# Low parts of the mixer's weights computed during the first feed-forward block and kept in DRAM

## The chip, the core and the metric

The kernel runs on one core of one Trainium2 chip. The metric is the device time of one execution in microseconds (us).

## The reference, cut to what matters

One layer of a decoder for 512 prompt tokens and 8 x 4 sample tokens, model width 1024: a feed-forward half step, a mixer, a second feed-forward half step, each followed by a layer norm.

```python
h = layer_norm(ALPHA * x + 0.5 * swiglu(x, ffn1_w_gate, ffn1_w_up, ffn1_w_down), ln1_g, ln1_b)
mixed, state = mix_fn(h, lw)            # projections by w_in, two head groups, projection by w_out
h = layer_norm(ALPHA * h + mixed, ln2_g, ln2_b)
y = layer_norm(ALPHA * h + 0.5 * swiglu(h, ffn2_w_gate, ffn2_w_up, ffn2_w_down), ln3_g, ln3_b)
```

swiglu(x) is (silu(x @ w_gate) * (x @ w_up)) @ w_down with a hidden width of 2816. The mixer's head groups are a state-space scan (SSD) and an attention with a compressed, a selected and a window branch. All of it is float32.

## The kernel before, in words

Every large matmul is made of three with fewer bits: a float32 operand is split into a high part (the value rounded to the type fp32r) and a low part (the value minus the high part), and `gemm` (lines 256 to 265) adds high x high, high x low and low x high in PSUM. Activations are split once, when they are made (`split`, lines 190 to 192). Weights are split each time they are used, by the class `Weights` (lines 149 to 172).

The weights are cut into units, mostly 128 x 8 x 128 values (512 KB; 128 partitions of 4 KB). The list `units` holds them in the order of use: 44 gate and up units and 24 down units of the first feed-forward block, the mixer's, then the second block's. `Weights.load` (line 160) issues a load of the next unit into `w_raw` (2 buffers) on SP's queue. `Weights.get` makes `w_hi` on ScalarE (line 170) and `w_lo` on VectorE, or on POOL where the caller says so (line 171); both have 3 buffers, so a unit's buffers are free when TensorE has finished with the unit three before it.

The mixer has 33 units: 20 projections of `w_in` (kc, vc, ks, kw, vs, vw, q0 to q3, x0 to x5, z0 to z3), one narrow one for dt and gates (`wdg`, 128 x 8 x 32), four of the key and value compression (c0 to c3) and eight of `w_out` (`wout`). The four c units are used twice, for the prompt and for the samples, so `get` is called 37 times in the mixer. The callers are `proj` (line 618 on; POOL makes the low part, except for kc), `compress_prompt` (POOL), `compress_sample` (VectorE) and the output projection in `mix` (`attention(d)`, VectorE). In the output projection the attention half of unit d+3 follows the other half of unit d.

The two feed-forward blocks are calls of one function, `ffn` (from line 367). For each of 22 f it takes a gate and a up unit, two token halves of 272 columns each, SiLU on ScalarE, the product on VectorE and a split of the product into hH and hL; then for each of 8 d it takes three down units, and VectorE, ScalarE and POOL make the residual and the sums for the norm (lines 272, 307 to 326, 421).

The order of each engine's queue is planned when the program is built, `tile.TileContext(nc, schedule_with_timeline_sim=True)`: the program's text gives ranks, and the planner follows a simulated time line and puts next into a queue what is ready then. On the chip each engine, and SP and POOL as issuers of DMAs, then runs its queue in that fixed order, waiting where something is late.

Of the kernel before, what the change touches and what calls it, by code (L numbers as in the profile page):

```python
# [25 lines left out]
F32 = mybir.dt.float32  # L26
F32R = mybir.dt.float32r
BF = mybir.dt.bfloat16
I32 = mybir.dt.int32
AF = mybir.ActivationFunctionType  # L30
OP = mybir.AluOpType
# [5 lines left out]
D, KD = 1024, 8  # L37
# [111 lines left out]
class Weights:  # L149


    def __init__(self, nc, pool, units, dma):
        self.nc, self.pool, self.units, self.dma, self.n = nc, pool, units, dma, 0
        self.raw = []

    def load(self):
        ap = self.units[self.n + len(self.raw)]
        _, nk, m = ap.shape
        raw = self.pool.tile([128, 8, 128], F32, name="w_raw", bufs=2)
        self.dma.dma_start(raw[:, :nk, :m], ap)  # L160
        self.raw.append(raw)

    def get(self, eng=None, pool=None):
        if not self.raw:
            self.load()
        nc, raw = self.nc, self.raw.pop(0)
        _, nk, m = self.units[self.n].shape
        self.n += 1
        hi, lo = ((pool or self.pool).tile([128, 8, 128], F32R, name=n, bufs=1 if pool else 3) for n in ("w_hi", "w_lo"))
        nc.scalar.activation(hi[:, :nk, :m], raw[:, :nk, :m], AF.Copy)  # L170
        (eng or nc.vector).tensor_tensor(lo[:, :nk, :m], raw[:, :nk, :m], hi.bitcast(F32)[:, :nk, :m], op=OP.subtract)  # L171
        return hi, lo


@with_exitstack
def step_kernel(ctx, tc, I, O, stop=99):
# [40 lines left out]

    ffn_units("1")
    seen = []
    for step in T0_ORDER + T1_ORDER + T2_ORDER:  # L220
        if step in ("c0", "c1", "c2", "c3"):
            units.append(I["w1"][int(step[1])])
        elif step == "dg":
            units.append(I["wdg"])
        elif step == "k" and seen.count("k") < 2:
            units.extend([I["w1"][seen.count("k") * 2 + i] for i in range(2)])
        elif step == "x":
            units.append(I["win"][IN_TILES.index(f"x{seen.count('x')}")])
        elif step in IN_TILES:
            units.append(I["win"][IN_TILES.index(step)])  # L230
        seen.append(step)
    units.extend([I["wout"][d] for d in range(KD)])
    ffn_units("2")
    W = Weights(nc, wpool, units, nc.sync)

    with tc.tile_pool(name="xload", bufs=1) as xp:

# [40 lines left out]
    class Norm:  # L278
# [3 lines left out]
        def __init__(self, pool, g, b, n, eps, to_x=True):  # L282
            self.g, self.b, self.eps, self.to_x = g, b, eps, to_x
            self.n = n
            self.m0 = pool.tile([128, 2, HT], F32, name="ln_m0")
            self.accS = keep.tile([128, 2, HT], F32, name=f"accS{n}", tag="accS")
            self.accQ = keep.tile([128, 2, HT], F32, name=f"accQ{n}", tag="accQ")
            self.y, self.rest = [], []
            self.extra_done = False
# [77 lines left out]
    def ffn(pre, post, last):  # L367

        with tc.tile_pool(name="ffn", bufs=1) as fp, tc.tile_pool(name="ffn_ps", bufs=1, space=PS) as pp:
            hH = fp.tile([128, KF, 2, HT], F32R, name="hH")  # L370
            hL = fp.tile([128, KF, 2, HT], F32R, name="hL")
            with tc.tile_pool(name="ffn_g", bufs=1) as gp:
                for f in range(KF):
                    sg = {}
                    for which in range(2):
                        wt = W.get()
                        cw = gp.tile([128, 2], F32, name="cw", bufs=4)
                        for h in range(2):
                            ps = pp.tile([128, 512], F32, name="mm", bufs=6)
                            rh, rl, n = xcols(h, pre is not None)  # L380
                            gemm(ps[:, :n], wt, (rh, rl), KD)
                            if f == 0 and which == 0 and h == 0 and pre is not None:
                                pre.stats(gp, pp)
                            if pre is None:
                                src = ps[:, :HT]
                            else:
                                src = gp.tile([128, HT], F32, name="fold_o", bufs=2)
                                pre.fold(ps, h, cw, src, gp)
                            if which == 0:
                                sg[h] = gp.tile([128, HT], F32, name="sg", bufs=3)  # L390
                                if pre is None:
                                    nc.scalar.activation(sg[h], src, AF.Silu)
                                else:
                                    nc.scalar.activation(sg[h], src, AF.Silu, bias=cw[:, 1:2])
                            else:
                                hf = gp.tile([128, HT], F32, name="hf", bufs=2)
                                if pre is None:
                                    nc.vector.tensor_tensor(hf, src, sg[h], op=MUL)
                                else:
                                    nc.vector.scalar_tensor_tensor(hf, src, cw[:, 1:2], sg[h], op0=ADD, op1=MUL)  # L400
                                split(hH[:, f, h], hL[:, f, h], hf)
            with tc.tile_pool(name="ffn_d", bufs=1) as dp:
                nrm = Norm(dp, *post, eps4, to_x=not last)

                tab = dp.tile([128, 1], F32, name="tab")
                nc.scalar.activation(tab, f32(hH)[:, KF - 1, 1, 0:1], AF.Sqrt, scale=0.0, bias=eps1)
                for d in range(KD):
                    t = dp.tile([128, 2, HT], F32, name="res", bufs=2)
                    if pre is None:
                        padd(t, f32(XH[d])[:, :, :HT], f32(XL[d])[:, :, :HT])  # L410
                    else:
                        pre.value(d, t, dp, nc.gpsimd)
                    ps = [pp.tile([128, 512], F32, name="mm", bufs=6) for _ in range(2)]
                    wts = [W.get() for _ in range(3)]

                    def down(i, h):
                        gemm(ps[h][:, :HT], wts[i], (lambda k: hH[:, k, h], lambda k: hL[:, k, h]),
                             min(8, KF - 8 * i), 8 * i, start=i == 0, stop=i == 2)

                    def residual(h):  # L420
                        nc.vector.scalar_tensor_tensor(t[:, h], t[:, h], 2.0 * ALPHA, ps[h][:, :HT],
                                                       op0=MUL, op1=ADD)

                    if d < KD - 1:
                        for i in range(3):
                            for h in range(2):
                                down(i, h)
                        for h in range(2):
                            residual(h)
                        if d == 0:  # L430
                            nrm.mean0(t, dp, pp)
                        nrm.tile(d, t, dp)
                    else:
                        for h in range(2):
                            for i in range(3):
                                down(i, h)
                            residual(h)
                            nrm.tile(d, t, dp, slice(h, h + 1))
                            if last:
                                nrm.stats(dp, pp, (h,))  # L440
                                for e in range(KD):
                                    u = dp.tile([128, HT], F32, name="fin_u", bufs=3)
                                    y = nrm.y[e][:, h]
                                    nc.scalar.activation(u, nrm.nmr[:, h], AF.Identity, scale=nrm.g[:, e:e + 1],
                                                         bias=nrm.b[:, e:e + 1])
                                    if e in (2, 5, 7):
                                        pmul(y, y, nrm.rstd[:, h])
                                        padd(y, y, u)
                                    else:
                                        nc.vector.tensor_tensor(y, y, nrm.rstd[:, h], op=MUL)  # L450
                                        nc.vector.tensor_tensor(y, y, u, op=ADD)
                                    nc.sync.dma_start(O["y"][h, :, e], y)
            return nrm
# [1042 lines left out]
```

## Time and profile before

| | before |
|---|---|
| median of 3 runs | 1320.4 us (1319.51 to 1321.38) |
| profiled execution: its own time, its span | 1316.73 us, 1315.0 us |
| mean granted TensorE clock | 0.975 |
| busy: TensorE, VectorE, ScalarE, POOL | 1250.2, 778.3, 479.1, 355.0 us |
| DMA moved | 126.74 MB, mean 96 GB/s |

PE is TensorE, DVE is VectorE, ACT is ScalarE, POOL is GpSimd, SP is SyncE, which computes nothing and issues DMAs. Times of the profile begin at the span's start. The first feed-forward block ends at about 410 us, the mixer at about 890 us, the second block at the end. The granted clock is given as a share of full speed. A wait row names the instruction that waited, after the arrow the one that ended the wait, and then the total, how often, and the longest.

### The profile page before, as it was taken

The numbers are of one execution on the slowest core, as the hardware profiler recorded it, in microseconds if no ns is written. First come the engines' busy times: TensorE is split into PE (matmuls) and PEld (weight loads), VectorE is DVE, ScalarE is ACT, GpSimd is POOL, SyncE is SP. The second block draws the span as 40 slices with busy tenths as digits, with TensorE's granted clock in tenths as the row PEclk, the third lists the DMA queues.
The fourth block names the chain that finished last, engine by engine and source line by source line (L and its number), as shares of the span: only waits on it lengthen the run. The fifth ranks groups of instructions, "written<-read, shape, count | busy, mean of one in ns | idle before, by whom it ended". The sixth has DMA issues, their size and how long they took to land.

```text
span 1315.0 us, 24300 instructions
## 1 busy us (share of the span) xinstructions
PE 1250.2 (95%) x9768; PEld 1178.3 (90%) x9768; DVE 778.3 (59%) x1510; ACT 479.1 (36%) x900; POOL 355.0 (27%) x289
## 2 busy tenths in 40 slices
PE   8999999999999888999999999779999999999994
PEld 7999999999999788888887676779999999999993
DVE  4333333334336888766798685997666666644446
ACT  4322223232224445454554332434333333342213
POOL 0000000001333653453555542770000000035543
PEclk9999999999999997999999998989999999999997
DMA  5222232222324324532232651222222232323211
GB/s 204 81 89 88 82 96 81 90 80 89 89 89 146 128 75 147 143 128 85 38 98 39 200 207 63 65 64 81 81 91 87 81 96 81 90 80 89 89 57 68
DMA packets 63888, 126.74 MB, mean 96 GB/s; under 512 B 16168, under 2 KB 35312, under 8 KB 63776
## 3 DMA queue, kind: packets, MB, share of 16 engines
q1 hardware_dynamic: 61040, 116.52, 29.3%
q0 software_dynamic: 1584, 4.48, 1.0%
q10 hardware_dynamic: 1152, 4.19, 0.8%
q8 instruction: 77, 1.26, 0.4%
q14 instruction: 35, 0.29, 0.1%
HBM read 114.80 MB, written 9.36 MB: 94 GB/s over the span
## 4 chain that ended last, share of the span: by engine, by line
PE 52%; DVE 7%; issue 1%; ACT 1%; DMA 1%; POOL 1%; ACTq 0%; POOLq 0%; DVEq 0%
PE mm L265 12%; PE mm L264 12%; PE mm L263 12%; PE pv L915 3%; PE pj L263 2%; PE pj L264 2%; PE pj L265 2%; PE tp L925 1%; PE sc L884 1%; PE sc L886 1%; DMA win<-in_vwin 1%; DVE XL L311 1%; DVE XL L326 1%; PE tp L1266 1%; PE sg L975 0%
## 5 line engine op out<-in xcount | busy, mean ns | idle before, releaser
L263 PE MATMUL mm<-XH,w_hi 128*128 128x272 f32 (+1 forms) x1408 | 409.1, 291 | 11.8 <-ACT XH L191 6.3
L265 PE MATMUL mm<-XH,w_lo 128*128 128x272 f32 (+1 forms) x1408 | 409.4, 291 | 0.0
L264 PE MATMUL mm<-XL,w_hi 128*128 128x272 f32 (+1 forms) x1408 | 408.4, 290 | 0.3 <-DVE XL L192 0.3
L171 DVE TENSOR_TENSOR w_lo<-w_raw,w_hi 128x1024 fp32r<-128x1024 f32 x149 | 183.6, 1232 | 205.1 <-ACT w_hi L170 203.4
L170 ACT ACTIVATE w_hi<-w_raw 128x1024 fp32r<-128x1024 f32 (+1 forms) x173 | 179.2, 1036 | 284.5 <-PE mm L264 231.9
L263 PEld LDWEIGHTS mm<-XH,w_hi 128*128 128x128 f32 x1408 | 268.1, 191 | 12.4 <-ACT XH L191 6.5
L264 PEld LDWEIGHTS mm<-XL,w_hi 128*128 128x128 f32 x1408 | 268.6, 191 | 0.7 <-DVE XL L192 0.6
L265 PEld LDWEIGHTS mm<-XH,w_lo 128*128 128x128 f32 x1408 | 267.4, 190 | 0.1
L265 PE MATMUL mm<-hH,w_lo 128*128 128x272 f32 x704 | 203.9, 290 | 0.0
L264 PE MATMUL mm<-hL,w_hi 128*128 128x272 f32 x704 | 203.4, 289 | 0.0
L263 PE MATMUL mm<-hH,w_hi 128*128 128x272 f32 x704 | 203.0, 288 | 0.0
L272 POOL TENSOR_TENSOR res<-XH,XL 128x544 f32<-128x544 f32 x24 | 35.0, 1468 | 588.9 <-DVE hL L192 550.0
L264 PEld LDWEIGHTS mm<-hL,w_hi 128*128 128x128 f32 x704 | 132.6, 188 | 0.2
L263 PEld LDWEIGHTS mm<-hH,w_hi 128*128 128x128 f32 x704 | 132.5, 188 | 0.1
L265 PEld LDWEIGHTS mm<-hH,w_lo 128*128 128x128 f32 x704 | 132.3, 188 | 0.2
L263 PE MATMUL pj<-XH,w_hi 128*128 128x272 f32 (+3 forms) x336 | 99.9, 297 | 7.0 <-DVE pj_u L640 5.8
L265 PE MATMUL pj<-XH,w_lo 128*128 128x272 f32 (+3 forms) x336 | 98.8, 294 | 0.0
L264 PE MATMUL pj<-XL,w_hi 128*128 128x272 f32 (+3 forms) x336 | 98.2, 292 | 0.0
L191 ACT ACTIVATE hH<-hf 128x272 fp32r<-128x272 f32 x88 | 37.5, 426 | 144.7 <-DVE hf L400 98.0
L263 PEld LDWEIGHTS pj<-XH,w_hi 128*128 128x128 f32 (+1 forms) x336 | 62.4, 186 | 11.2 <-issue 7.3
L321 POOL TENSOR_TENSOR accS<-res,accS 128x544 f32<-128x544 f32 x18 | 35.7, 1982 | 121.5 <-DVE res L307 121.5
L171 POOL TENSOR_TENSOR w_lo<-w_raw,w_hi 128x1024 fp32r<-128x1024 f32 (+1 forms) x24 | 56.8, 2365 | 38.4 <-ACT w_hi L170 38.4
(423 smaller groups left out, 2146.8 us busy)
## 6 DMA issues: line engine op xcount, KB each, us to landing
w_raw<-in_wg SPq DMA_DIRECT2D x44, 512.0 KB, 3.5
w_raw<-in_wu SPq DMA_DIRECT2D x44, 512.0 KB, 3.5
w_raw<-in_wd SPq DMA_DIRECT2D x32, 512.0 KB, 3.5
w_raw<-in_win SPq DMA_DIRECT2D x20, 512.0 KB, 3.6
pg<-in_cmp SPq DMA_DIRECT2D x64, 128.0 KB, 2.4
w_raw<-in_wd SPq DMA_DIRECT2D x16, 384.0 KB, 3.1
w_raw<-in_w SPq DMA_DIRECT2D x8, 512.0 KB, 3.7
pg<-in_kslc SPq DMA_DIRECT2D x64, 64.0 KB, 1.9
```

Source lines behind the costliest of these rows:

```text
L170: nc.scalar.activation(hi[:, :nk, :m], raw[:, :nk, :m], AF.Copy)
L171: (eng or nc.vector).tensor_tensor(lo[:, :nk, :m], raw[:, :nk, :m], hi.bitcast(F32)[:, :nk, :m], op=OP.subtract)
L191: nc.scalar.activation(hi, src, AF.Copy)
L263: nc.tensor.matmul(ps, hi[:, k, :m], rh(k0 + k), start=b, stop=False)
L264: nc.tensor.matmul(ps, hi[:, k, :m], rl(k0 + k), start=False, stop=False)
L265: nc.tensor.matmul(ps, lo[:, k, :m], rh(k0 + k), start=False, stop=e)
L272: nc.gpsimd.tensor_tensor(out, a, b, op=ADD)
L311: nc.vector.scalar_tensor_tensor(XL[d][:, h, :HT], s[:, h], self.g[:, d:d + 1], f32(XH[d])[:, h, :HT], op0=MUL, op1=SUB)
L321: eng.tensor_tensor(acc[:, h], v[:, h], acc[:, h], op=ADD)
L326: nc.vector.tensor_tensor(XL[d][o], col[:, d:d + 1], f32(XH[d])[o], op=SUB)
L884: nc.tensor.matmul(s, q, S.K[:, br, h // 4, 0, :w], start=True, stop=False)
L915: nc.tensor.matmul(pv[hh * 64:hh * 64 + 64, hp % 2], v, t[:, hh], start=start, stop=stop)
```

## The change

- The mixer's 33 units get names (`c0`, `dg`, `kc`, `x0`, `o0` and so on), and the list holds the names in place of the arrays.
- A new class, `Ahead`, has one DRAM tile of 512 KB for each of the 33. Its generator `run` loads a unit's array on POOL's queue into `a_raw` (3 buffers, two loads issued ahead), makes the high part on ScalarE (`a_hi`, 1 buffer), subtracts it in place on VectorE and stores the low part to DRAM on POOL's queue.
- `ffn` steps that generator in the first block only: once for each of the 22 f, once or twice for each of the 8 d (12 in all). The first step only loads; the other 33 make one unit each.
- `Weights.get` makes `w_hi` of a named unit on ScalarE as before and loads `w_lo` from DRAM on SP's queue in place of the subtraction.

```diff
     def load(self):
         ap = self.units[self.n + len(self.raw)]
+        if isinstance(ap, str):
+            ap = self.ahead.units[ap]
         _, nk, m = ap.shape
         raw = self.pool.tile([128, 8, 128], F32, name="w_raw", bufs=2)
         self.dma.dma_start(raw[:, :nk, :m], ap)
...
         nc.scalar.activation(hi[:, :nk, :m], raw[:, :nk, :m], AF.Copy)
+        if name:
+            self.dma.dma_start(lo.bitcast(F32)[:, :nk, :m], self.ahead.rest[name][:, :nk, :m])
+            return hi, lo
         (eng or nc.vector).tensor_tensor(lo[:, :nk, :m], raw[:, :nk, :m], hi.bitcast(F32)[:, :nk, :m], op=OP.subtract)
         return hi, lo
+
+class Ahead:
+    def __init__(self, nc, pool, units):
+        self.nc, self.units, self.rest = nc, units, {}
+        self.dram = {n: pool.tile([128, 8, 128], F32, name=f"rest_{n}") for n in units}
+
+    def run(self, pool):
+        nc, names, raws = self.nc, list(self.units), []
+        todo = iter(names)
+
+        def load():
+            n = next(todo, None)
+            if n is None:
+                return
+            _, nk, m = self.units[n].shape
+            raw = pool.tile([128, 8, 128], F32, name="a_raw", bufs=3)
+            nc.gpsimd.dma_start(raw[:, :nk, :m], self.units[n])
+            raws.append(raw)
+
+        load()
+        load()
+        yield
+        for n in names:
+            raw = raws.pop(0)
+            _, nk, m = self.units[n].shape
+            hi = pool.tile([128, 8, 128], F32R, name="a_hi", bufs=1)
+            nc.scalar.activation(hi[:, :nk, :m], raw[:, :nk, :m], AF.Copy)
+            nc.vector.tensor_tensor(raw[:, :nk, :m], raw[:, :nk, :m], hi.bitcast(F32)[:, :nk, :m], op=OP.subtract)
+            nc.gpsimd.dma_start(self.dram[n][:, :nk, :m], raw[:, :nk, :m])
+            self.rest[n] = self.dram[n]
+            load()
+            yield
...
             hL = fp.tile([128, KF, 2, HT], F32R, name="hL")
+            side = ahead.run(fp) if pre is None else iter(())
             with tc.tile_pool(name="ffn_g", bufs=1) as gp:
                 for f in range(KF):
+                    next(side, None)
...
                 for d in range(KD):
+                    for _ in range(1 + d % 2):
+                        next(side, None)
                     t = dp.tile([128, 2, HT], F32, name="res", bufs=2)
```

The arithmetic is the same, but for the low part's type: it is kept as float32 where it was rounded to fp32r.

## Rows read from the trace of the kernel before

**Rows 1.** Stages: stretch, length, busy us of each engine (instructions), granted clock, DMA share, GB/s.

```profile
33.00:400.00 367.00, 367.00 (x2901) 366.84 (x2900) 131.53 (x190) 106.34 (x177) 33.48 (x20) 1.00 0.28 87
410.00:510.00 100.00, 84.11 (x626) 80.22 (x624) 87.02 (x147) 49.48 (x88) 53.55 (x35) 0.96 0.44 136
510.00:540.00 30.00, 28.45 (x182) 26.69 (x183) 23.28 (x50) 16.50 (x42) 9.43 (x9) 0.74 0.55 157
540.00:820.00 280.00, 273.14 (x2256) 213.07 (x2255) 204.36 (x561) 120.65 (x303) 133.45 (x141) 0.98 0.37 108
820.00:890.00 70.00, 54.06 (x365) 51.07 (x365) 64.59 (x79) 28.58 (x56) 48.62 (x28) 0.91 0.21 65
```

**Rows 2.** Waits of PE, 410 to 540 us, then (after the dots) 820 to 892 us.

```profile
PE pj L263 <- DVE pj_u L640: 5.8, 5, 1.7
PE mm L264 <- DVE cL L192: 3.8, 1, 3.8
...
PE acc L263 <- DVE res L607: 8.0, 3, 3.0
PE mm L263 <- DVE res L607: 5.6, 1, 5.6
```

**Rows 3.** Groups by line, 403 to 892 us, DVE and POOL: busy us, mean ns.

```profile
L171 DVE TENSOR_TENSOR w_lo<-w_raw,w_hi 128x1024 fp32r<-128x1024 f32 x16 | 21.9, 1371 | 1.1 <-ACT w_hi L170 1.0
...
L171 POOL TENSOR_TENSOR w_lo<-w_raw,w_hi 128x1024 fp32r<-128x1024 f32 x23 | 56.0, 2436 | 38.4 <-ACT w_hi L170 38.4
```

**Rows 4.** Time lines of DVE and POOL, 419 to 504 us: start, duration.

```profile
420.45 2.15 DVE L343 TENSOR_TENSOR ln_mq<-ln_mq 128x272 f32<-128x272 f32 x1 [0.17 <-ACT ln_mq L341]
...
457.97 2.12 DVE L791 TENSOR_TENSOR sp_a<-sp_a,sp_b 128x40 f32<-128x40 f32 x1
460.12 0.20 DVE L792 TENSOR_TENSOR sp_b<-sp_a 128x40 f32<-128x40 f32 x1
...
499.92 3.45 DVE L192 TENSOR_TENSOR K<-pj_f,K 64x512 fp32r<-64x512 f32 x2
...
419.90 2.40 POOL L171 TENSOR_TENSOR w_lo<-w_raw,w_hi 128x1024 fp32r<-128x1024 f32 x1 [6.10 <-ACT w_hi L170]
...
457.64 2.39 POOL L171 TENSOR_TENSOR w_lo<-w_raw,w_hi 128x1024 fp32r<-128x1024 f32 x1 [2.08 <-ACT w_hi L170]
...
500.48 2.35 POOL L171 TENSOR_TENSOR w_lo<-w_raw,w_hi 128x1024 fp32r<-128x1024 f32 x1 [0.90 <-ACT w_hi L170]
```

**Rows 5.** DVE in the output projection, 830 to 890 us: group, then two of its time line.

```profile
L171 DVE TENSOR_TENSOR w_lo<-w_raw,w_hi 128x1024 fp32r<-128x1024 f32 x8 | 11.0, 1378 | 0.0
...
833.61 1.47 DVE L171 TENSOR_TENSOR w_lo<-w_raw,w_hi 128x1024 fp32r<-128x1024 f32 x1
...
870.71 1.22 DVE L171 TENSOR_TENSOR w_lo<-w_raw,w_hi 128x1024 fp32r<-128x1024 f32 x1
```

**Rows 6.** DMA issues of the whole run: count, KB each, median us to landing.

```profile
w_raw<-in_wg SPq DMA_DIRECT2D x44, 512.0 KB, 3.5
...
out_kwin<-win ACTq DMA_DIRECT2D x4, 512.0 KB, 2.8
out_vwin<-win ACTq DMA_DIRECT2D x4, 512.0 KB, 6.8
...
vp<-in_vslc,vrow POOLq DMA_INDIRECT x8, 7.5
```

**Rows 7.** Groups in the first feed-forward block: DVE 33 to 270, ACT 33 to 400.

```profile
L171 DVE TENSOR_TENSOR w_lo<-w_raw,w_hi 128x1024 fp32r<-128x1024 f32 x39 | 47.8, 1225 | 97.5 <-ACT w_hi L170 97.5
...
L170 ACT ACTIVATE w_hi<-w_raw 128x1024 fp32r<-128x1024 f32 x54 | 57.3, 1061 | 124.2 <-PE mm L264 95.0 <-issue 25.6 <-PE mm L265 2.8
```

**Rows 8.** The start: POOL's time line, a stretch of 2 us, DMA issues until 40 us.

```profile
3.09 0.58 POOL L533 DMA_DIRECT2D mk_c<-in_cst  x1
...
6.00:8.00 2.00, 1.46 (x5) 1.16 (x6) 2.00 (x5) 1.16 (x4) 0.00 (x0) 1.00 1.04 381
...
xr<-in_x SPq DMA_DIRECT2D x4, 544.0 KB, 6.6
```

More of the change, by code (lines that the diff above doesn't have):

```diff
@@ L149, with __init__ @@
 class Weights:
-    def __init__(self, nc, pool, units, dma):
+    def __init__(self, nc, pool, units, dma, ahead):
         self.nc, self.pool, self.units, self.dma, self.n = nc, pool, units, dma, 0
         self.raw = []
+        self.ahead = ahead
     def load(self):
         ap = self.units[self.n + len(self.raw)]
+        if isinstance(ap, str):
+            ap = self.ahead.units[ap]
         _, nk, m = ap.shape
@@ L166, in get @@
         nc, raw = self.nc, self.raw.pop(0)
-        _, nk, m = self.units[self.n].shape
+        ap = self.units[self.n]
+        name = ap if isinstance(ap, str) else None
+        _, nk, m = (self.ahead.units[name] if name else ap).shape
         self.n += 1
@@ L219, in step_kernel, with unit @@
     seen = []
+    named = {}
+    def unit(name, ap):
+        named[name] = ap
+        units.append(name)
     for step in T0_ORDER + T1_ORDER + T2_ORDER:
         if step in ("c0", "c1", "c2", "c3"):
-            units.append(I["w1"][int(step[1])])
+            unit(step, I["w1"][int(step[1])])
         elif step == "dg":
-            units.append(I["wdg"])
+            unit(step, I["wdg"])
         elif step == "k" and seen.count("k") < 2:
-            units.extend([I["w1"][seen.count("k") * 2 + i] for i in range(2)])
+            units.extend(f"c{seen.count('k') * 2 + i}" for i in range(2))
         elif step == "x":
-            units.append(I["win"][IN_TILES.index(f"x{seen.count('x')}")])
+            unit(f"x{seen.count('x')}", I["win"][IN_TILES.index(f"x{seen.count('x')}")])
         elif step in IN_TILES:
-            units.append(I["win"][IN_TILES.index(step)])
+            unit(step, I["win"][IN_TILES.index(step)])
         seen.append(step)
-    units.extend([I["wout"][d] for d in range(KD)])
+    for d in range(KD):
+        unit(f"o{d}", I["wout"][d])
     ffn_units("2")
-    W = Weights(nc, wpool, units, nc.sync)
+    ahead = Ahead(nc, ctx.enter_context(tc.tile_pool(name="rests", bufs=1, space=bass.MemoryType.DRAM)), named)
+    W = Weights(nc, wpool, units, nc.sync, ahead)
     with tc.tile_pool(name="xload", bufs=1) as xp:
```

## The prediction

> **What bounds the kernel now.** I read the stages by time first [rows 1]. From 33 to 400 us, in the first feed-forward block, TensorE is busy 367.0 of 367.0 us at full clock. Nothing there can become faster; it can only be disturbed. VectorE (131.5 us), ScalarE (106.3) and the DMA engines (share 0.28) have room. The mixer is different. From 410 to 510 us TensorE is idle for 15.9 us while VectorE is busy 87.0 of 100, and from 820 to 890 us it is idle for 15.9 us while VectorE is busy 64.6 of 70. The granted clock is below 1 in the same places: 0.96, 0.74 (510 to 540), 0.91. Full speed minus granted, times the stretch, is 4.0 + 7.8 = 11.8 us up to 540 and 6.3 us from 820 to 890. The middle, 540 to 820, loses 6.9 us idle and 5.6 us of clock in 280.
>
> The waits of TensorE say who is late [rows 2]: up to 540 us VectorE's projection outputs (5.8 us) and a split that stands in its queue (3.8); in the output projection VectorE's residual additions (8.0 and 5.6 us).
>
> What the low parts cost is in the groups [rows 3]. POOL makes 23 full ones in the mixer (and one small), 56.0 us in all. VectorE's 16 in that stretch, 21.9 us, are 13 of the mixer and the first 3 of the second feed-forward block. POOL's cost falls on VectorE too, which the two time lines show side by side [rows 4]. A 128x40 operation of VectorE that starts at 457.97, just after POOL's low part at 457.64, lasts 2.12 us; the like operation behind it lasts 0.20. From the low part at 419.90 to the one at 500.48 there are 12; beside 11 of them a VectorE operation is stretched like this. I took off from each what its line takes undisturbed: 0.9 to 2.2 us each, 19.9 us together.
>
> **The change part by part.** The sum is made against the profiled execution: span 1315.0 us, own time 1316.7. The median of the runs shown, 1320.4, is 3.7 above it.
>
> *Up to 540 us.* VectorE loses 19.9 us of stretching and five low parts ("kc" and the four of the sample compression) at the 1.37 of [rows 3], 6.9; that is 27 of its 110.3 busy us. The bound below is 0, if the chains behind TensorE's waits are late for another reason; the bound above is all idle and clock loss, 17.4 + 11.8 = 29.2. I take two thirds of the named waits on VectorE (two thirds of 14.6, the sum of all of them in this stretch, 9.6 of which stand in [rows 2], is 10) and nearly half of the clock loss (5), since the clock is low right behind the idle time: **−15**.
>
> *From 540 to 820 us.* TensorE is busy 273 of 280. Ten POOL low parts (x and z) go; bounds 0 and −12.5; I take **−2**.
>
> *Output projection.* VectorE makes eight low parts from 830 to 890 us, 11.0 us [rows 5]; the first five (833.61 to 870.71) are of the output weights, 6.6 us, and go; the last three are of the feed-forward block and stay. VectorE is the bound, so up to 6.6 us go directly; with the clock up to 6.6 + 6.3 = 13. I take **−6**.
>
> *The new loads in the mixer.* 37 loads of 512 KB on SP, each waiting for its w_lo buffer, which is free when TensorE has finished three units back. Behind a waiting load in SP's queue stand the next raw load, page and window loads and output stores; TensorE would see them late. A unit is 6.1 us of matmuls (48 at 367 us for 2901, [rows 1]), so two units, 12 us, lie between the buffer and its use. The price of a 512 KB load is 3.5 us on a quiet queue and 7.5 in a crowded stretch [rows 6], within the 12. ScalarE's copy and POOL's low part took 1.06 + 2.44, so the load comes no later than what it replaces. Only in the output projection is it short: main part d frees the buffer that attention part d+3 needs some 3 us later. There copy plus subtraction took about 2.4 us and the load takes 3.5; half a microsecond for five units, some contention: **+2** (0 to 20, the upper end from 7.5 us five times).
>
> *The first feed-forward block.* Added are 33 ScalarE copies (1.06 us [rows 7]), 33 subtractions (1.23), 33 loads and 33 stores on POOL's queue, each with an issue time like that of POOL's DMAs, 0.6 us [rows 8]. 33 x 1.06 = 35 us fit beside ScalarE's 106 of 367, and 33 x 1.23 = 41 beside VectorE's 132. The 34.6 MB at some 370 GB/s, the rate at 6 to 8 us, are 94 us of the DMA engines, beside 0.28 of 367. So capacity covers all of it; what is not covered is order. The pace in the text (one unit for each f) only ranks instructions. The planner issues what is ready, as mk_c shows [rows 8]: a load that the text places after the whole block is issued at 3.09 us. So I expect the three raw buffers to be filled at the start, and the 33 units to run as fast as those three buffers turn, well before the middle of the block. Per unit the chain is load, copy, subtraction, store: quiet, 3.5 + 1.06 + 1.23 + 2.8 = 8.6, over three buffers 2.9 us; crowded, 7.5 + 1.06 + 1.23 + 6.8 = 16.6, or 5.5 us. ScalarE's queue is fixed: a copy whose load is late holds the next w_hi and the SiLU behind it, and TensorE waits for those once three prepared units (12 us) are used up. A few such places: **+4** (0, if the plan has the loads right, up to the 75 of the third rival). No row shows a 512 KB load from POOL on a quiet queue. [...]
>
> *Start.* From 6 to 8 us the DMA engines' share is 1.04 at 381 GB/s [rows 8], and x, which the first matmuls need, lands 6.6 us after its issue. Three side loads, 1.57 MB, take 4.2 us of these engines; two take 2.8. Bounds 0 and 4.2; I take **+3**, since TensorE is fed by x all through this stretch. [...]
>
> Sum: −15 − 2 − 6 + 2 + 4 + 3 = −14. 1316.7 − 14 = 1302.7 for a profiled execution, and with the 3.7 us that the median stands above it **1306 us**.
>
> **The rivals.** *More than that:* VectorE's waits vanish and the clock holds. Then up to 540 us 24 of 29 come back, in the output projection 10, in the middle 4; against +5 at the start and in the block this is −33, 1287 us. For it: two stages in which VectorE is the only full engine. Against it: the rotary and K chains stay serial.
>
> *Nothing:* the waits change hands. The load stands where the subtraction stood, SP is held by buffers and brings pages later, and TensorE waits for DMA, some 15 us in place of my 2: −1, about 1319 us. For it: SP runs further ahead today than it could behind such loads. Against it: TensorE waits on no weight load in [rows 2].
>
> *Slower:* the side chain runs behind its plan in the first block. If the plan counts on 2.9 us a unit and the chip needs 5.5, the queue of ScalarE is 33 x 2.6 = 86 us late, less 12 of prepared units: 75. Halfway it is 43 − 12, some 32 us, in place of my +4. With the mixer's −21 and the start's +3 that gives 1320.4 + 14, 1334 us. It decides from (12 + 18) / 33 = 0.9 us of delay per unit. For it: the loads of weights and the side chain together want (1.05 MB per 2.9 us, and 0.52 per 6.1) some 447 GB/s, more than the 381 of [rows 8]. Against it: a plan that knows of the shared rate sets the copies later.
>
> That the change does not do what it says (evenly) I count as likely, and it is in the forecast already; evenly spread, the +4 would be 0.
>
> **How the numbers follow.** Forecast 0.50, with its own range 1296 to 1316; more 0.18; nothing 0.12; slower 0.20. About 0.2%, 2.6 us, is what a measurement of this kernel can tell from no change. Faster: 0.50 + 0.18, and a little of "nothing", 0.70. Same 0.08. Slower 0.20 and a little of "nothing", 0.22. The range runs from 1285, just below the second case, to 1328, where most of the slower one is left out.
>
> **What would show it.** Right: from 410 to 510 us VectorE below 70 busy, no operation of 40 columns above 0.5 us, TensorE idle below 8; from 820 to 890 the stage about 6 us shorter; POOL's busy time in the mixer down by 56. The side copies bunched before 200 us would show the planner's order; spread to 400, that I misread it. Wrong: a busy share of TensorE below 1 between 33 and 400 us, with ScalarE's copies or w_hi waiting on a side load (the third rival); or waits of TensorE on w_lo loads (the second).

## The result, and the profile after

| | before | after |
|---|---|---|
| median | 1319.95 us (4 runs, 1318.42 to 1321.38) | 1301.82 us (4 runs, 1299.09 to 1307.62) |
| profiled execution: its own time, its span | 1316.73, 1315.0 us | 1301.37, 1299.6 us |
| mean granted TensorE clock | 0.975 | 0.980 |
| busy: TensorE, VectorE, ScalarE, POOL | 1250.2, 778.3, 479.1, 355.0 us | 1244.7, 769.2, 509.1, 335.2 us |
| DMA moved | 126.74 MB | 179.59 MB |

After takes 0.9869 of the time before, 95% interval 0.9833 to 0.9904: faster by some 18 us. The forecast was 1306 us, in a range of 1285 to 1328.

To compare stages between kernels I cut every profile at the same five events: the last residual addition of the first feed-forward block, the first softmax operation of the prompt attention, the second gated normalisation of the state-space output, the first reciprocal of the norm behind the output projection, and VectorE's last addition to y. These are the stages of after in the table of stretches (length; busy time of TensorE, of its weight loads, of VectorE, ScalarE and POOL; granted clock, DMA share, GB/s); before had 410.5, 117.9, 295.7, 71.6 and 415.0 us.

```profile
0.00:415.20 415.20, 406.20 (x3172) 404.42 (x3172) 184.17 (x259) 154.96 (x245) 71.66 (x93) 1.00 0.53 177
415.20:517.30 102.10, 97.90 (x695) 94.94 (x696) 73.55 (x163) 57.53 (x108) 27.89 (x25) 0.90 0.73 232
517.30:813.10 295.80, 286.23 (x2369) 224.26 (x2369) 204.48 (x590) 129.80 (x328) 120.38 (x138) 0.99 0.44 136
813.10:878.20 65.10, 55.96 (x414) 54.09 (x413) 60.46 (x78) 29.69 (x57) 44.98 (x28) 0.97 0.35 114
878.20:1290.80 412.60, 398.38 (x3124) 396.24 (x3122) 245.99 (x444) 136.60 (x198) 69.22 (x47) 0.99 0.26 82
...
33.00:400.00 367.00, 364.59 (x2871) 363.34 (x2870) 160.92 (x219) 132.59 (x206) 62.00 (x78) 1.00 0.51 170
410.00:510.00 100.00, 95.80 (x695) 92.84 (x693) 71.46 (x157) 56.55 (x103) 26.76 (x24) 0.92 0.74 231
510.00:540.00 30.00, 28.43 (x218) 26.45 (x217) 18.87 (x48) 15.10 (x37) 13.38 (x11) 0.92 0.67 212
```

In the order of time: the first block is 4.7 us longer, the first mixer stretch 15.8 shorter, the middle the same, the output projection 6.5 shorter, the last block 2.4 shorter; and the span ends 8.8 us after VectorE's last addition to y, where it was 4.3. Together that is -15.4, the difference of the spans. The last three rows answer to [rows 1]: from 410 to 510 us VectorE is busy 71.5 us in place of 87.0 and TensorE idle 4.2 in place of 15.9. From 33 to 400 us TensorE is now idle for 2.4 us, where it was idle for none, and gets through 30 matmuls fewer (2871 in place of 2901), 3.8 us at the pace of before.

The waits of TensorE: up to 420 us (the first 6.3 us are the wait for x, which was there before), then 410 to 540, then 813 to 880.

```profile
PE mm L314 <- ACT XH L234: 6.3, 1, 6.3
PE mm L316 <- DVE w_lo L179: 1.9, 2, 0.9
...
PE mm L315 <- POOL cs_L L1250: 1.6, 1, 1.6
PE pj L314 <- DVE pj_u L695: 1.0, 1, 1.0
PE pj L316 <- DMA w_lo<-rest_dg: 0.5, 1, 0.5
...
PE mm L314 <- DVE res L662: 3.7, 1, 3.7
PE acc L314 <- DVE res L662: 2.4, 2, 1.4
```

Against [rows 2], pj_u went from 5.8 to 1.0, the wait for cL is gone, and the residual waits went from 8.0 and 5.6 to 2.4 and 3.7. The new loads of w_lo cost TensorE 0.5 us, once.

The time line of VectorE in the same stretch holds the operations that [rows 4] showed stretched:

```profile
425.76 0.44 DVE L394 TENSOR_TENSOR ln_mq<-ln_mq 128x272 f32<-128x272 f32 x1 [0.18 <-ACT ln_mq L392]
456.68 0.73 DVE L697 TENSOR_TENSOR pj_u<-pj_u,pj_b 128x544 f32<-128x544 f32 x1
457.75 0.20 DVE L846 TENSOR_TENSOR sp_a<-sp_a,sp_b 128x40 f32<-128x40 f32 x1
```

What took 2.15 and 2.12 us takes 0.44 and 0.20.

ScalarE's waits up to 420 us show the side chain:

```profile
ACT a_hi L210 <- DMA a_raw<-in_win: 38.2, 14, 5.5
ACT a_hi L210 <- DMA a_raw<-in_wout: 14.3, 7, 4.3
ACT a_hi L210 <- DMA a_raw<-in_w: 6.5, 4, 3.0
```

The 33 copies run from 19 to 168 us, not spread to the block's end at 410, and ScalarE waits 59 us in all for their loads. The first three of these loads are issued together, at 15 us, after a wait for VectorE (first row). How a late load reaches TensorE shows at 162 us: a copy waits for its load, the w_hi behind it in ScalarE's queue is late, and a matmul waits for that.

```profile
15.35 1.61 POOL L200 DMA_DIRECT2D a_raw<-in_win  x3 [12.22 <-DVE XL L235]
...
162.01 1.06 ACT L210 ACTIVATE a_hi<-a_raw 128x1024 fp32r<-128x1024 f32 x1 [2.35 <-DMA a_raw<-in_wout]
162.97 1.04 ACT L175 ACTIVATE w_hi<-w_raw 128x1024 fp32r<-128x1024 f32 x1
...
164.07 0.39 PE L314 MATMUL mm<-XH,w_hi 128*128 128x272 f32 x1 [0.43 <-ACT w_hi L175]
```

### The profile page after: what moved, and what is told of

Same layout as the page of the kernel before. It is cut to its first block, busy times and chain, and to the rows that moved or that the text cites. A ratio compares the mean times of both kernels' runs of the same rounds, so it can differ in the third digit from the quotient of the medians.

```text
span 1299.6 us, 24524 instructions
## 1 busy us (share of the span) xinstructions
PE 1244.7 (96%) x9768; PEld 1173.9 (90%) x9768; DVE 769.2 (59%) x1530; ACT 509.1 (39%) x933; POOL 335.2 (26%) x331
## 2 busy tenths in 40 slices
DMA packets 79426, 179.59 MB, mean 138 GB/s; under 512 B 18840, under 2 KB 37984, under 8 KB 79312
## 4 chain that ended last, share of the span: by engine, by line
PE 75%; DMA 10%; DVE 7%; issue 4%; ACT 2%; SPq 1%; POOL 1%; ACTq 0%; POOLq 0%; DVEq 0%
PE mm L316 18%; PE mm L315 18%; PE mm L314 18%; DMA a_raw<-in_win 3%; PE pj L316 3%; PE pj L314 3%; PE pv L970 3%; PE pj L315 2%; PE tp L980 1%; PE sc L939 1%; DMA out_sconv<-hist_s 1%; PE sc L941 1%; DVE a_raw L211 1%; DMA a_raw<-in_wout 1%; ACT a_hi L210 1%
## 5 line engine op out<-in xcount | busy, mean ns | idle before, releaser
L314 PE MATMUL mm<-XH,w_hi 128*128 128x272 f32 (+1 forms) x1408 | 409.4, 291 | 10.4 <-ACT XH L234 6.3
L179 DVE TENSOR_TENSOR w_lo<-w_raw,w_hi 128x1024 fp32r<-128x1024 f32 (+1 forms) x136 | 167.2, 1229 | 144.4 <-ACT w_hi L175 142.9
L234 ACT ACTIVATE hH<-hf 128x272 fp32r<-128x272 f32 x88 | 37.6, 427 | 134.0 <-DVE hf L453 97.5
L211 DVE TENSOR_TENSOR a_raw<-a_raw,a_hi 128x1024 f32<-128x1024 f32 (+1 forms) x33 | 39.6, 1200 | 62.5 <-ACT a_hi L210 62.5
L316 PEld LDWEIGHTS pj<-XH,w_lo 128*128 128x128 f32 (+1 forms) x336 | 63.3, 188 | 3.6 <-issue 2.1
```

Of the source, the lines that this page charges most:

```text
L211: nc.vector.tensor_tensor(raw[:, :nk, :m], raw[:, :nk, :m], hi.bitcast(F32)[:, :nk, :m], op=OP.subtract)
L234: nc.scalar.activation(hi, src, AF.Copy)
L314: nc.tensor.matmul(ps, hi[:, k, :m], rh(k0 + k), start=b, stop=False)
L316: nc.tensor.matmul(ps, lo[:, k, :m], rh(k0 + k), start=False, stop=e)
```

## The experiments

All stages in us, cut as above. "Side DMAs" are the transfers of the side chain that POOL issues.

| kernel | side DMAs | first block | first stretch | middle | output | last block | end | ratio to before (95%) |
|---|---|---|---|---|---|---|---|---|
| before | 0 | 410.5 | 117.9 | 295.7 | 71.6 | 415.0 | 4.3 | |
| after | 66 | 415.2 | 102.1 | 295.8 | 65.1 | 412.6 | 8.8 | 0.9869 (0.9833 to 0.9904) |
| after, again | 66 | 419.1 | 96.2 | 298.9 | 65.0 | 412.6 | 8.8 | 0.9896 (0.9870 to 0.9921) |
| POOL's work back | 66 | 419.8 | 114.9 | 303.9 | 65.1 | 414.8 | 8.8 | 1.0105 (1.0067 to 1.0143) |
| all on VectorE, no DRAM | 0 | 410.6 | 108.5 | 291.5 | 69.1 | 412.7 | 4.2 | 0.9868 (0.9837 to 0.9899) |
| 15 units | 30 | 411.9 | 97.1 | 298.7 | 69.2 | 414.8 | 5.9 | 0.9836 (0.9800 to 0.9873) |
| 8 units | 16 | 410.6 | 121.0 | 297.8 | 64.1 | 412.7 | 4.7 | 0.9953 (0.9928 to 0.9979) |
| two a_raw | 66 | 418.9 | 97.4 | 298.2 | 65.1 | 412.6 | 8.8 | 0.9892 (0.9865 to 0.9918) |
| side chain on SP | 0 | 410.4 | 95.3 | 300.4 | 65.1 | 412.6 | 4.3 | 0.9801 (0.9770 to 0.9832) |
| its loads on SP | 33 | 410.7 | 99.8 | 306.9 | 65.2 | 412.7 | 6.1 | 0.9790 (0.9764 to 0.9815) |
| 8 units, rest on VectorE | 16 | 410.3 | 107.6 | 303.0 | 66.2 | 412.7 | 4.7 | 0.9916 (0.9890 to 0.9942) |
| 23 units, rest on VectorE | 46 | 412.9 | 97.7 | 293.6 | 64.4 | 414.9 | 7.2 | 0.9836 (0.9819 to 0.9852) |
| the same, side chain on SP | 0 | 411.5 | 102.2 | 294.2 | 63.8 | 414.8 | 4.2 | 0.9743 (0.9720 to 0.9765) |

The stages are those of one profiled execution of each kernel, which can stand well off its median: with the loads on SP it took 1303.12 us, the median is 1294.82. The middle alone runs from 291.5 to 306.9 us in this table.

### POOL's subtraction put back as dead work

```diff
             self.dma.dma_start(lo.bitcast(F32)[:, :nk, :m], self.ahead.rest[name][:, :nk, :m])
+            if eng is nc.gpsimd:
+                eng.tensor_tensor(raw[:, :nk, :m], raw[:, :nk, :m], hi.bitcast(F32)[:, :nk, :m], op=OP.subtract)
             return hi, lo
```

> The kernel after, with POOL's subtraction put back as dead work: for every mixer unit that POOL used to split, POOL subtracts w_hi from w_raw in place and nobody reads the result (w_lo still comes from DRAM). If POOL's low parts cost VectorE its time (my theory), the stretch from the end of the first feed-forward block to the first softmax of the prompt attention, 118.0 us before and 102.1 after, goes back to 112 to 118, VectorE operations of 40 columns of about 2 us come back beside the subtractions, and the whole takes 1311 to 1318 us. If the gain came from VectorE's own five low parts or from w_lo being ready earlier (the rival), the stretch stays at 102 to 104 and the whole at about 1302.

Measured: 1331.38 us (1328.10 to 1337.79), ratio 1.0105; the first stretch takes 114.9 us. The stretch came as expected, the whole did not: the first block (419.8 us) and the middle (303.9) came out longer as well. The stretch's row, and the group of POOL's subtractions in it (busy us, mean ns):

```profile
419.80:534.70 114.90, 99.81 (x696) 96.02 (x697) 97.45 (x164) 56.01 (x107) 56.53 (x38) 0.88 0.65 209
...
L179 POOL TENSOR_TENSOR w_raw<-w_raw,w_hi 128x1024 f32<-128x1024 f32 (+1 forms) x13 | 30.4, 2335 | 18.8 <-ACT w_hi L175 16.7 <-POOL pj_f L328 0.9 <-POOL w_raw L179 0.8
```

VectorE is busy 97.5 us with 164 instructions, in after 73.6 with 163. Nobody reads what POOL computes here; so 23.9 us of VectorE's time are stretching by 13 operations of POOL, 1.8 us each. The time lines show two of the pairs, with the neighbour of the second pair undisturbed:

```profile
464.63 2.37 POOL L179 TENSOR_TENSOR w_raw<-w_raw,w_hi 128x1024 f32<-128x1024 f32 x1 [4.89 <-ACT w_hi L175]
467.79 2.39 POOL L179 TENSOR_TENSOR w_raw<-w_raw,w_hi 128x1024 f32<-128x1024 f32 x1 [0.80 <-POOL w_raw L179]
...
464.64 2.94 DVE L699 TENSOR_TENSOR pj_u<-pj_u,pj_b 128x544 f32<-128x544 f32 x1
467.92 2.31 DVE L848 TENSOR_TENSOR sp_a<-sp_a,sp_b 128x40 f32<-128x40 f32 x1
470.27 0.20 DVE L849 TENSOR_TENSOR sp_b<-sp_a 128x40 f32<-128x40 f32 x1
```

In both pairs the VectorE operation starts just after POOL's (464.64 us against 464.63, and 467.92 against 467.79) and ends only after POOL's has ended (467.58 against 467.00, and 470.23 against 470.18), the one of 544 columns as the one of 40; the next behind the second takes 0.20 us. What holds the operation up, these rows don't name.

TensorE's longest waits in the stretch are those of before again [rows 2], on VectorE; for a weight it waits 0.3 us, once, so the dead work does not act by making weights late:

```profile
PE pj L316 <- DVE pj_u L697: 4.9, 5, 1.7
PE mm L317 <- DVE cL L237: 3.8, 1, 3.8
```

What follows: POOL's work put back takes the stretch from 102.1 us (96.2 in after's second execution, below) to 114.9, so 12.8 to 18.7 us hang on it. The 3.0 us between that and the 117.9 of before, in which VectorE's own five low parts lie, are too few to be read from one profile of each.

### All low parts on VectorE, none in DRAM

```diff
-        (eng or nc.vector).tensor_tensor(lo[:, :nk, :m], raw[:, :nk, :m], hi.bitcast(F32)[:, :nk, :m], op=OP.subtract)
+        nc.vector.tensor_tensor(lo[:, :nk, :m], raw[:, :nk, :m], hi.bitcast(F32)[:, :nk, :m], op=OP.subtract)
```

(in the kernel before)

> The kernel before, nothing kept in DRAM, with one change: VectorE makes every low part, POOL none. If POOL's low parts cost VectorE more (19.9 us of stretching up to 540 us) than making them costs it (11 of 1.37 = 15 us), the first mixer stretch gets slightly shorter than 118.0 us, 112 to 118, and the whole is 1314 to 1321 us. If the stretching is an accident of what else ran then, VectorE, busy 87 of 100 there, only gets 15 us more to do: the stretch is 126 to 134 us and the whole 1328 to 1340.

Measured: 1299.84 us (1298.41 to 1306.20), ratio 0.9868. The expectation missed on the good side: the whole was to take 1314 to 1321 us, and the first stretch (first row) is 108.5 us, where I had 112 to 118. The second row is VectorE's group of low parts in it:

```profile
410.60:519.10 108.50, 99.58 (x723) 96.91 (x723) 91.72 (x184) 59.34 (x112) 29.23 (x23) 0.91 0.46 140
...
L171 DVE TENSOR_TENSOR w_lo<-w_raw,w_hi 128x1024 fp32r<-128x1024 f32 (+1 forms) x17 | 21.6, 1269 | 4.6 <-ACT w_hi L170 4.5
```

VectorE makes 17 low parts here for 21.6 us and is still busy 9.6 us less than before (101.4 in this stretch). A one-line edit thus buys as much as the whole change. Keeping low parts in DRAM adds a shorter first stretch and output projection and takes about as much back elsewhere.

### Low parts in DRAM for some units only

```diff
     def unit(name, ap):
+        if name[0] in "xzo":
+            units.append(ap)
+            return
         named[name] = ap
```

> The kernel after, with low parts kept in DRAM only for the 15 units of the first mixer stage; x, z and the output units are split as before. If the stages are independent, the first mixer stretch keeps its gain (102 us against 118.0), the output projection its old length (71.6), the first block loses 15/33 of 4.8, some 2 us, and the end after the last y addition (4.3 before, 8.8 after) is 6.3 if it grows with the number of POOL's DMAs; whole 1306 to 1309. If the x and z units of the middle carry something, the middle (295.7 us in both) gets longer or shorter than that. If the end does not depend on POOL's DMAs, it is 4.3 or 8.8.

With `if name[0] != "o"` in its place:

> The kernel after, with low parts kept in DRAM only for the 8 output units. If the stages are independent: first mixer stretch 118 us, output projection 65 us (71.6 before, 65.1 after), first block +1, end 5.4 if it grows with POOL's DMAs; whole 1313 to 1316. If the output projection was shorter only because what came before it ran otherwise (the clock, the order), it stays at 71 and the whole at 1320.

Measured: 15 units 1299.81 us (1292.40 to 1300.75), better than expected, with the first stretch at 97.1 us; 8 units 1313.10 us (1309.01 to 1315.97), the output projection at 64.1. So the output projection's gain is its own, and the ten x and z units carry nothing that shows: the middle is 298.7 us without them and 295.8 and 298.9 with them. The end grows with POOL's transfers: 4.3, 4.7, 5.9, 8.8 us for 0, 16, 30, 66. In the 8-unit kernel the first stretch, in which no instruction was edited, came out 3 us longer than before; differences of that size between two plans I don't read.

### The side chain's pace and its queue

```diff
-            raw = pool.tile([128, 8, 128], F32, name="a_raw", bufs=3)
+            raw = pool.tile([128, 8, 128], F32, name="a_raw", bufs=2)
```

> The kernel after with two buffers for a_raw in place of three. A unit of the side chain (load 5.5, copy 1.1, subtraction 1.2, store 5 us) then turns in about 6.5 us in place of 4.6, and the 33 units end near 230 us in place of 170, with a lower DMA share beside them than 0.84 to 0.89. If the first block's 4.8 us come from the crowd on the DMA engines, which makes w_raw and a_raw loads late, the block ends at 411 to 413 us (415.2 after, 410.5 before) and the whole is about 1298. If they come from ScalarE's queue holding copies that the plan sets too early for the chip, whatever the crowd (the rival), fewer buffers make each copy later still: the block ends at 416 to 425 us and the whole is 1303 to 1311. Everything behind the block as in after.

```diff
-            nc.gpsimd.dma_start(raw[:, :nk, :m], self.units[n])
+            nc.sync.dma_start(raw[:, :nk, :m], self.units[n])
...
-            nc.gpsimd.dma_start(self.dram[n][:, :nk, :m], raw[:, :nk, :m])
+            nc.sync.dma_start(self.dram[n][:, :nk, :m], raw[:, :nk, :m])
```

> The kernel after with the side chain's 33 loads and 33 stores issued on SP's queue in place of POOL's. If the 4.5 us between the last work and the end of the span (8.8 us after the last y addition, 4.3 before) belong to the number of DMAs that POOL has issued, the end is 4.3 to 4.6 us again. If they belong to the number of DMAs, or to the 33 DRAM tiles, it stays 8.8. In the first block a side load or store that waits now holds the weight loads behind it on SP: 415 to 422 us, against 415.2; if the side chain's waits were all short, 411 to 415. Whole 1296 to 1304 with the short end.

With the first of these two edits alone:

> The kernel after with the side chain's 33 loads on SP's queue and its 33 stores on POOL's as they were. If the end grows with the number of DMAs that POOL issues, it is about 6.3 to 6.6 us, halfway between 4.3 and 8.8. If the first block's 4.8 us come from side loads that POOL issues past the weight loads in SP's order, the block ends at 410 to 412 as with all of them on SP; if from the stores, at 414 to 419.

Measured: two buffers 1305.43 us (1302.75 to 1309.58), the block at 418.9; all on SP 1292.80 us (1289.89 to 1298.94), below the expected range, the block at 410.4 and the end at 4.3; loads on SP 1294.82 us (1290.63 to 1303.12), the block at 410.7 and the end at 6.1. The waits up to 420 us of ScalarE and TensorE, first with two buffers, then with the chain on SP, then TensorE's in the second execution of after (three buffers):

```profile
ACT a_hi L210 <- DMA a_raw<-in_win: 49.4, 16, 5.3
ACT a_hi L210 <- DMA a_raw<-in_wout: 30.5, 6, 6.5
ACT a_hi L210 <- DMA a_raw<-in_w: 12.0, 4, 4.6
PE mm L316 <- DVE w_lo L179: 3.3, 4, 1.3
PE mm L314 <- ACT w_hi L175: 1.8, 1, 1.8
```

```profile
ACT a_hi L210 <- DMA a_raw<-in_win: 29.8, 14, 5.0
ACT a_hi L210 <- DMA a_raw<-in_wout: 17.9, 8, 5.0
ACT a_hi L210 <- DMA a_raw<-in_w: 7.6, 3, 3.9
PE mm L314 <- ACT XH L234: 6.5, 1, 6.5
```

```profile
PE mm L316 <- DVE w_lo L179: 4.6, 5, 1.1
PE mm L314 <- ACT w_hi L175: 2.2, 1, 2.2
```

With two buffers the crowd on the DMA engines is thinner (share between 0.5 and 0.9 in each 10 us from 30 to 220 us, where after has 0.78 to 0.95 from 30 to 170), and that did not bring the block back to 411 to 413 us. That later copies hurt, the rival of that expectation, is not shown either: ScalarE waits 92 us for a_raw in place of 59, but TensorE waits 5.1 us for weights and the block ends at 418.9, while after with its three buffers has 2.3 us and 415.2 in one execution and 6.8 us and 419.1 in the other. More hangs on the queue, or on the plan that comes with it: with the loads on SP, alone or with the stores, TensorE waits for no weight, although ScalarE still waits 53 and 56 us for side loads. Moving the stores changes nothing in the block (410.7 against 410.4). POOL's loads did not land later: the median landing of the 20 loads of w_in is 5.5 us from POOL in after and 6.0 from SP with the chain there. What stays open is whether the queue itself or the other plan that comes with it keeps the copies within the cover; I changed both at once. ScalarE's order did change: its first copies and high parts stand as copy, w_hi, copy, copy in after and as copy, copy, w_hi, copy with the chain on SP.

The end settles: 33 side DMAs on POOL give 6.1 us, 66 give 8.8, and none 4.3, with the same number of DMAs and DRAM tiles.

### The kernel after once more

> The kernel after once more, to see what of a stage belongs to the kernel and what to one execution. Belonging to the kernel, by my reading: the first block's end at 415 (within 1), the output projection's 65.1, the end's 8.8. Open: the two stretches at half clock in the first mixer stretch (455 to 465 us at 0.57, 505 to 515 at 0.51), where a kernel with the same TensorE instructions and SP's queue had one. If they belong to the kernel, the stretch is 102 again and its clock 0.90; if to the execution, it is 95 to 98 with a clock of 0.93 to 0.96, and about 5 us of the gain that I had forecast from the clock are there in some executions only.

Measured: 1306.16 us (1302.38 to 1310.05). Of my readings the output projection (65.0) and the end (8.8) hold; the first block doesn't (419.1). The first stretch is 96.2 us, first row; then two places of this execution, the first with the 10 us ahead of it, and after them the same in the first execution:

```profile
419.10:515.30 96.20, 91.45 (x695) 88.36 (x696) 73.93 (x163) 57.49 (x107) 27.23 (x25) 0.96 0.78 246
...
449.00:459.00 10.00, 8.35 (x65) 7.63 (x64) 7.92 (x19) 7.65 (x15) 3.29 (x3) 1.00 0.48 159
459.00:469.00 10.00, 10.00 (x83) 10.00 (x83) 8.83 (x35) 4.24 (x6) 1.01 (x2) 1.00 0.76 247
509.00:519.00 10.00, 10.00 (x75) 9.78 (x75) 6.34 (x13) 5.26 (x11) 3.28 (x2) 0.83 0.86 291
```

```profile
445.00:455.00 10.00, 8.32 (x58) 7.59 (x57) 7.91 (x18) 7.86 (x15) 3.48 (x3) 0.92 0.47 158
455.00:465.00 10.00, 10.00 (x52) 10.00 (x51) 5.21 (x22) 2.84 (x5) 0.00 (x0) 0.57 0.69 235
505.00:515.00 10.00, 10.00 (x49) 9.91 (x49) 4.78 (x13) 5.72 (x17) 0.37 (x1) 0.51 0.99 327
```

In the first execution TensorE's granted clock is 0.57 and 0.51 in the two places, and it gets through 52 and 49 matmuls. The second ran the first place at 1.00, with 83. What the engine did before was much alike: in the 10 us ahead it was busy 8.3 and 8.4 us, with 58 and 65 matmuls (the fall begins there in the first execution, 0.92), and in the 10 us before that 9.1 and 9.5. The same program thus has one such fall or two, and the clock takes 3.8 us of the stretch in the one case and 10.2 in the other, about the difference between 96.2 and 102.1; a stage of one profile is known no better than that.

### Versions of both

Low parts on VectorE by the edit of the second experiment, and in DRAM for the units named:

> A version of both: low parts from DRAM for the 8 output units only, and every other low part of the mixer on VectorE, none on POOL. If the stages add up: first block 410.6, first mixer stretch 108.5 and middle 291.5 (as with all low parts on VectorE), output projection 64 to 65 (as with the 8 units kept), last block 412.7, end 4.7; whole about 1294 (1290 to 1298). If the order that the planner finds matters more than these terms, it is 1299 or above.

> A version of both: low parts from DRAM for the 15 units of the first mixer stage and the 8 output units; the ten x and z units are split on VectorE, none on POOL. If the stages add up: first block 412.5, first mixer stretch 97 to 102, middle 291.5, output projection 64 to 65, last block 412.7, end 7; whole about 1289 (1284 to 1295). If the middle's gain with all low parts on VectorE (291.5 against 295.7) came from the stage ahead of it, the middle is 295 to 299 and the whole 1293 to 1297.

With the side chain on SP as well:

> What the runs so far point to: low parts from DRAM for the 15 units of the first stage and the 8 output units, x and z units split on VectorE, and the side chain's loads and stores on SP's queue. If the stages add up: first block 410.4, first mixer stretch and middle together 391 (as with these 23 units on POOL's queue), output projection 64.4, last block 413 to 415, end 4.3; span 1285 and a median of 1288 to 1293. If the order on SP, with fewer side transfers, is another than with 33 units, the first block or the middle is longer and the median 1295 to 1300.

Measured: 8 units 1308.77 us (1306.28 to 1312.69), 23 units 1298.38 us (1292.45 to 1300.65), 23 units with SP 1286.69 us (1285.80 to 1292.45). The first missed: its middle is 303.0 us in place of the 291.5 that had come with all low parts on VectorE, so the middle's terms don't add from one plan to the next. The second missed too, above both of its ranges, though its profiled execution was the fastest of the five (1292.45). The last came in just below its range and is the fastest kernel here, 0.9743 of before (0.9720 to 0.9765), some 34 us, and its interval lies wholly below that of after. Its first two stages:

```profile
0.00:411.50 411.50, 404.74 (x3172) 404.05 (x3172) 174.14 (x250) 146.26 (x235) 35.50 (x27) 1.00 0.47 153
411.50:513.70 102.20, 98.00 (x695) 95.05 (x696) 73.47 (x163) 57.49 (x107) 27.84 (x25) 0.90 0.75 231
```

The first block is within 1 us of the one before. The first stretch has the clock of 0.90 that after had with both falls, and this profiled execution, 1292.45 us, is the slowest of the five.

## Why the prediction was right

The total was right, 1301.8 against 1306, and so was the reason that carried most of it: POOL's low parts held up VectorE, and VectorE held up TensorE. By its terms:

- *Up to 540 us, -15.* Measured -15.8, and -21.7 in the second execution. That POOL's low parts cost VectorE its time was the ground of it. The 19.9 us that I summed from eleven pairs, 1.8 each, hold: measured are 23.9 us for 13, 1.8 each. The split of the term was off: TensorE's idle time fell by 11.6 us (17.4 to 5.8) where I had 10, but of the 5 us of clock the profiled execution gave back 1.4 (11.8 to 10.4). The second one shows that they can come: 0.04 of 96.2 is a loss of 3.8 us, against 10.2 in the first (0.10 of 102.1).
- *540 to 820 us, -2.* Measured +0.1 and +3.2. Ten POOL operations went and nothing came of it; the value taken was near the right end of its bounds.
- *Output projection, -6.* Measured -6.5, and 2.4 more in the last block, most of which is only a shift of 17 matmuls across the cut (3141 to 3124; 2.2 us at 6.1 us for 48). Alone, the 8 units give 64.1 us.
- *New loads, +2.* TensorE waited 0.5 us for one. The 7.5 us that I had for a crowded 512 KB load were misread: that row is of indirect loads whose size it doesn't give [rows 6]; the new loads of the x and z units landed in 3.6 and 3.3 us. The two units of cover held; the rival "nothing", with SP held by buffers, fell.
- *First block, +4.* Measured +4.7 and +8.6 for this and the next term together. The mechanism was named (a fixed queue on ScalarE, a late load that holds the next w_hi, TensorE late when the prepared units are used up), and its sign of being wrong, a busy share below 1 with w_hi behind a side load, showed at a small price; the rows at 162 us are such a place. The units turned in 4.6 us each (32 from 19.4 to 168.0 us), between my 2.9 and 5.5. What the term lacked is what makes such a wait cost something: with the loads on SP 53 and 56 us of ScalarE's waits cost nothing, with two buffers 92 us cost no more than 59 and 63 do in after, and which of queue and plan decides is open. The rival "slower", the same mechanism at a larger price, would have cost 32 us at half of its delay; it cost 5 to 9.
- *Start, +3.* Wrong: up to 33 us TensorE is busy 26.5 us before and 26.4 in after, with 192 matmuls before, 184 in after and 194 in the run with POOL's work back, so nothing to 1 us. No run shows the 3 us, an estimate from the rate at 6 to 8 us. The step that failed is "the three raw buffers to be filled at the start": a_raw takes over memory of the x tiles, and the first side loads waited 12 us for VectorE to finish with x before they were issued, at 15 us.
- *Not in the sum.* The end, +4.5 us. No row of before could show it: the end there is 4.3 us, without the side chain's transfers.

Summed up: the mixer and the last block gave 24.6 us where I had 21 with the new loads, the first block with its start cost 4.7 where I had 7, and the end cost 4.5 where I had nothing. That is -3.6 - 2.3 + 4.5 = -1.4, between -14 and -15.4: the total is nearer than the terms, and that an end which no term had takes up what the others gave beyond their price is luck. The other 3 us between 1306 and 1301.8 are the 3.7 by which the median of before stood above its profiled execution; in after that is 0.5, in its second measurement 3.8. Of what was to be seen, two signs were missed by little: VectorE came out at 71.5 busy, just above the 70 named, and one operation of 40 columns took 0.66 us, the others at most 0.40. Idle time below 8 was right (4.2). POOL's busy time in the mixer fell by 51, not 56. That the side copies bunch before 200 us was right.

## What to carry to other kernels

When an engine's short operations take ten times as long as their neighbours (here 2.31 us against 0.20), look at what the engine beside it started just before; the price of a helper is the time it takes from the engine that is full, and here 30 us of help on POOL cost VectorE 24. Before building storage for precomputed operands, try the one-line version: making them on the engine that was being "relieved" gave the same time. When work is then moved ahead, try its transfers on the queue whose order already holds the loads they compete with (here that block lost nothing, with the plan changed as well), and look at the whole span, its end too.

## What was not expected of the hardware

- The span's end grows with the DMAs that POOL has issued in the program, though the side chain's last one is issued at 171 us: 4.2 to 4.3 us with none of the side chain on POOL, 4.7 with 16, 5.9 with 30, 6.1 with 33, 7.2 with 46, 8.8 with 66. Nothing in the trace names what runs there: the last operation of after starts at 1291.42 us and takes 0.76, its span ends at 1299.6.
- One program has one fall of TensorE's clock in the first mixer stretch in one execution and two in another, with the same instructions. What decides it was not tried.
